# Carrying a part of the rows of a column roll through SBUF beside HBM to HBM copies

## The chip, the cores and the metric

The kernel runs on one core of a Trainium2 chip. The metric is the device time of one execution in microseconds (us): a median of 828.96 us over 3 runs (828.69 to 829.57) before the change. One further execution was taken with the hardware profiler; its span, from the first to the last instruction, is 815.4 us, and its own time is 817.17 us.

## What is computed

```python
def setup_inputs():
    return {"x": np.random.randn(8192, 8192).astype(np.float32), "shift": 100}

def reference(x, shift):
    return np.roll(x, shift, axis=1)
```

Every row of 8192 floats (32,768 B) is shifted right by 100 columns. The last 100 values of a row, its wrapped end, come to stand at the front of the same row. Nothing is calculated: 268 MB are read from the chip's memory (HBM) and 268 MB are written to it.

## The kernel before, in words

With shift 100 the kernel has `s = 100`, `a = 128` (the shift rounded up to 128 columns, so that writes start at a multiple of 512 B) and `g = a - s = 28`. It cuts every output row into two parts.

The **body** is columns 128 to 8191 of the output, 8064 values or 32,256 B of each row, which are columns 28 to 8091 of the input. It is copied straight from HBM to HBM by 16 DMA instructions (lines 30 to 37). The views `xm` and `om` order the rows as (c, e, j): e has 16 values, one for each DMA engine, and j has 4. Each instruction takes one j and a quarter of the c values, that is 32 x 16 rows or 16.5 MB; one packet is one row of 32,256 B. The instructions go in turn to two DMA rings, that of the Sync engine (SP) and that of ScalarE (ACT).

The **ends** are columns 0 to 127 of the output: 100 wrapped values and the first 28 values of the input row. [...]lines 54 to 76 build them in SBUF. In each of two groups of 4096 rows, three DMA instructions on the GpSimd (POOL) queue (line 67) read 128 values across each row boundary (the end of one row and the start of the next lie side by side in memory), two more fetch what the boundaries inside the group don't give (lines 68 and 71), and VectorE (DVE) sorts the values into whole 512 B ends with two copies (lines 69 and 72). Four DMA instructions (line 76) then store the ends. All loads of both groups are issued before the first store: the stores stand in a loop of their own.

Within one engine's queue, instructions are issued one after the other. Tile, the layer that the kernel is written in, orders the instructions and sets the semaphores between them. The pools `reads` and `heads` have a buffer for each group, so no load waits for a store.

The 16 body copies wait for no data. The only thing that holds them back is how many may be under way.

Of the kernel before, what the change touches and what calls it, by code (L numbers as in the profile page):

```python
# [1 line left out]

# [4 lines left out]


@with_exitstack
def kernel(  # L10
    ctx: ExitStack,
    tc: tile.TileContext,
    x: bass.AP,
    shift: int,
    out: bass.AP,
):
    nc = tc.nc
    n_rows, n_cols = x.shape
    s = shift % n_cols
    a = -(-s // 128) * 128  # L20
    g = a - s
    P = nc.NUM_PARTITIONS
    engines = [nc.sync, nc.scalar]
    n_chunks = 16
    rows = n_rows // n_chunks

    xm = x.rearrange("(c e j) w -> j e c w", e=16, j=4)  # L30
    om = out.rearrange("(c e j) w -> j e c w", e=16, j=4)
    depth = n_rows // 64 // 4
    for c in range(4):
        for j in range(4):
            if a < n_cols:
                cs = slice(c * depth, (c + 1) * depth)
                engines[j % 2].dma_start(out=om[j, :, cs, a:], in_=xm[j, :, cs, g:n_cols - s])
    if a == 0:
        return


    if a > 512:
        for i in range(n_chunks):
            r = slice(i * rows, (i + 1) * rows)
            nc.gpsimd.dma_start(out=out[r, :s], in_=x[r, n_cols - s:])
            if g > 0:
                nc.gpsimd.dma_start(out=out[r, s:a], in_=x[r, :g])
        return

    Q, J = 4, 8
    n_st = n_rows // (P * Q * J)
    reads = ctx.enter_context(tc.tile_pool(name="reads", bufs=n_st))
    heads = ctx.enter_context(tc.tile_pool(name="heads", bufs=n_st))
    xt = x.rearrange("(k p j q) c -> k q p j c", q=Q, j=J, p=P)
    ot = out.rearrange("(k p j q) c -> k q p j c", q=Q, j=J, p=P)
    tiles = []  # L60
    for k in range(n_st):
        t = reads.tile([P, Q - 1, J, a], x.dtype)
        h = heads.tile([P, Q, J, a], x.dtype)
        for q in range(1, Q):
            lead = bass.AP(tensor=x.tensor, offset=(k * P * J * Q + q) * n_cols - s,
                           ap=[[J * Q * n_cols, P], [Q * n_cols, J], [1, a]])
            nc.gpsimd.dma_start(out=t[:, q - 1], in_=lead)  # L67
        nc.gpsimd.dma_start(out=h[:, Q - 1, :, :s], in_=xt[k, Q - 1, :, :, n_cols - s:])  # L68
        nc.vector.tensor_copy(h[:, :Q - 1, :, :s], t[:, :, :, :s])  # L69
        if g > 0:  # L70
            nc.gpsimd.dma_start(out=h[:, 0, :, s:], in_=xt[k, 0, :, :, :g])  # L71
            nc.vector.tensor_copy(h[:, 1:, :, s:], t[:, :, :, s:])  # L72
        tiles.append(h)
    for k, h in enumerate(tiles):
        for q in range(Q):
            nc.gpsimd.dma_start(out=ot[k, q, :, :, :a], in_=h[:, q])  # L76


# [1 line left out]
_INS = ['x', 'shift']  # L80
_OUTS = [((8192, 8192), 'float32')]

_NUMBERS = {'shift': 100}


# [26 lines left out]
```

## Time and profile before

| What | Value |
|---|---|
| Median time | 828.96 us |
| Span of the profiled execution | 815.4 us |
| VectorE busy | 3.7 us in 4 instructions |
| GpSimd busy | 16.1 us in 22 instructions |
| Body copies | 16 instructions of 16,128 KB, median 401.3 us (SP) and 400.5 us (ACT) from issue to landing |
| Loads for the ends | 6 of 512 KB, 118.2 us to landing; 2 of 400 KB, 151.3 us; 2 of 112 KB, 146.1 us |
| Stores of the ends | 8 of 512 KB, 182.5 us to landing |
| Last stores of the ends issued | 241.7 us |

How to read it: the time to landing of a DMA counts from its issue, so a copy that stands behind three others in its ring has a long one without being slow itself. The profile gives the DMA engines' busy share and the bytes that they moved in each stretch of the span. It counts a copy from HBM to HBM once in its GB/s, although HBM both reads and writes those bytes; for the total of HBM, reads and writes are added. A stretched packet counts as busy time, so a share of 1.00 does not tell whether the engines move data at their full rate.

### The profile page before, as it was taken

The numbers are of one execution on the slowest core, as the hardware profiler recorded it, in microseconds if no ns is written. First come the engines' busy times: TensorE is split into PE (matmuls) and PEld (weight loads), VectorE is DVE, ScalarE is ACT, GpSimd is POOL, SyncE is SP. The second block draws the span as 40 slices with busy tenths as digits, with TensorE's granted clock in tenths as the row PEclk, the third lists the DMA queues.
The fourth block names the chain that finished last, engine by engine and source line by source line (L and its number), as shares of the span: only waits on it lengthen the run. The fifth ranks groups of instructions, "written<-read, shape, count | busy, mean of one in ns | idle before, by whom it ended". The sixth has DMA issues, their size and how long they took to land. (4 is left out here: it accounts for less than half of the span.)

```text
span 815.4 us, 93 instructions
## 1 busy us (share of the span) xinstructions
DVE 3.7 (0%) x4; POOL 16.1 (2%) x22
## 2 busy tenths in 40 slices
DVE  0000000000000000000000000000000000000000
POOL 3000001000010000000000000000000000000000
DMA  9999999999999999999999999999999999999996
GB/s 310 341 328 347 330 349 335 337 340 346 338 337 346 338 348 348 347 333 345 340 344 337 349 326 335 334 329 334 335 329 331 329 335 334 332 331 332 329 334 250
DMA packets 10784, 272.63 MB, mean 334 GB/s; under 512 B 544, under 2 KB 544, under 8 KB 2592
## 3 DMA queue, kind: packets, MB, share of 16 engines
q10 hardware_dynamic: 4224, 132.12, 47.0%
q1 hardware_dynamic: 4224, 132.12, 46.9%
q0 software_dynamic: 2336, 8.39, 4.5%
HBM read 268.44 MB, written 268.44 MB: 658 GB/s over the span
## 5 line engine op out<-in xcount | busy, mean ns | idle before, releaser
L76 POOL DMA_DIRECT2D out_dram<-h x8 | 6.9, 954 | 170.1 <-DMA h<-in_x_dram 144.1
L67 POOL DMA_DIRECT2D t<-in_x_dram x6 | 5.4, 910 | 0.8 <-PEq L107 0.8
L69 DVE COPY h<-t 128x2400 f32<-128x2400 f32 x2 | 2.8, 1410 | 208.5 <-DMA t<-in_x_dram 208.5
L71 POOL DMA_DIRECT2D h<-in_x_dram x2 | 1.8, 883 | 28.6 <-DMA t<-in_x_dram 28.6
L68 POOL DMA_DIRECT2D h<-in_x_dram x2 | 1.8, 882 | 27.0 <-DMA t<-in_x_dram 27.0
L72 DVE COPY h<-t 128x672 f32<-128x672 f32 x2 | 1.0, 503 | 0.0
L93 POOL MEMSET const-float32-0.0<- 128x1 f32 x1 | 0.1, 99 | 0.2 <-issue 0.2
L93 POOL MEMSET const-bfloat16-1.0<- 128x1 bf16 x1 | 0.1, 103 | 0.0
L93 POOL MEMSET const-float32-1.0<- 128x1 f32 x1 | 0.1, 99 | 0.0
L93 POOL MEMSET const-uint8-127<- 128x1 uint8 x1 | 0.1, 99 | 0.0
## 6 DMA issues: line engine op xcount, KB each, us to landing
out_dram<-in_x_dram SPq DMA_DIRECT2D x8, 16128.0 KB, 401.3
out_dram<-in_x_dram ACTq DMA_DIRECT2D x8, 16128.0 KB, 400.5
out_dram<-h POOLq DMA_DIRECT2D x8, 512.0 KB, 182.5
t<-in_x_dram POOLq DMA_DIRECT2D x6, 512.0 KB, 118.2
h<-in_x_dram POOLq DMA_DIRECT2D x2, 400.0 KB, 151.3
h<-in_x_dram POOLq DMA_DIRECT2D x2, 112.0 KB, 146.1
```

The lines of the kernel that those rows point to most:

```text
L67: nc.gpsimd.dma_start(out=t[:, q - 1], in_=lead)
L68: nc.gpsimd.dma_start(out=h[:, Q - 1, :, :s], in_=xt[k, Q - 1, :, :, n_cols - s:])
L69: nc.vector.tensor_copy(h[:, :Q - 1, :, :s], t[:, :, :, :s])
L71: nc.gpsimd.dma_start(out=h[:, 0, :, s:], in_=xt[k, 0, :, :, :g])
L72: nc.vector.tensor_copy(h[:, 1:, :, s:], t[:, :, :, s:])
L76: nc.gpsimd.dma_start(out=ot[k, q, :, :, :a], in_=h[:, q])
L93: nc = _bacc.Bacc("TRN2", target_bir_lowering=False, num_devices=1)
```

## The change

The rows are divided. The last 1536 rows (3 batches of 128 partitions with 4 rows each) no longer take the copy and the ends. Each batch is loaded whole into SBUF, 4 rows or 131,072 B in a partition, at an offset of 100 values. VectorE then moves each row's last 100 values to the place in front of that row: four copies of 128x100 values for a batch. Because the rows lie side by side, the place in front of a row is where the end of the row before it stood, which has been moved by then. After that, one store from the start of the buffer writes the rolled rows. Loads and stores go on ACT's ring, cut into blocks of 16 KB. The pool `rows` has one buffer, so the batches follow one another.

The other 6656 rows keep the body copies, now all on SP's ring: 16 instructions of 26 x 16 rows each. Their ends are built as before, in two groups of 4096 and 2560 rows (J = 8 and 5), but each group's stores now stand right behind its own loads in the program text, and the batches' loads, copies and stores stand ahead of everything else.

What it is for: part of the traffic takes a way on which reads and writes go through SBUF as separate transfers on a ring of their own, and whose ends cost no short packets.

```diff
-    engines = [nc.sync, nc.scalar]
-    n_chunks = 16
-    rows = n_rows // n_chunks
+    per = 4
+    batches = 3
+    top = n_rows - batches * P * per
...
-    xm = x.rearrange("(c e j) w -> j e c w", e=16, j=4)
-    om = out.rearrange("(c e j) w -> j e c w", e=16, j=4)
-    depth = n_rows // 64 // 4
-    for c in range(4):
-        for j in range(4):
-            if a < n_cols:
-                cs = slice(c * depth, (c + 1) * depth)
-                engines[j % 2].dma_start(out=om[j, :, cs, a:], in_=xm[j, :, cs, g:n_cols - s])
+    pool = ctx.enter_context(tc.tile_pool(name="rows", bufs=1))
+    W = per * n_cols
+
+    def load(b):
+        r = slice(top + b * P * per, top + (b + 1) * P * per)
+        t = pool.tile([P, W + s], x.dtype)
+        nc.scalar.dma_start(out=t[:, s:], in_=x[r].rearrange("(p j) c -> p (j c)", j=per),
+                            max_dma_last_dim=16384)
+        return t
+
+    def store(b, t):
+        r = slice(top + b * P * per, top + (b + 1) * P * per)
+        for j in range(per):
+            if s > 0:
+                nc.vector.tensor_copy(t[:, j * n_cols:j * n_cols + s], t[:, (j + 1) * n_cols:(j + 1) * n_cols + s])
+        nc.scalar.dma_start(out=out[r].rearrange("(p j) c -> p (j c)", j=per), in_=t[:, :W],
+                            max_dma_last_dim=16384)
+
+    for b in range(batches):
+        store(b, load(b))
...
+    xm = x[:top].rearrange("(c e j) w -> j e c w", e=16, j=4)
+    om = out[:top].rearrange("(c e j) w -> j e c w", e=16, j=4)
+    if a < n_cols:
+        for c in range(0, top // 64, 26):
+            for j in range(4):
+                nc.sync.dma_start(out=om[j, :, c:c + 26, a:], in_=xm[j, :, c:c + 26, g:n_cols - s])
...
-    Q, J = 4, 8
-    n_st = n_rows // (P * Q * J)
-    reads = ctx.enter_context(tc.tile_pool(name="reads", bufs=n_st))
-    heads = ctx.enter_context(tc.tile_pool(name="heads", bufs=n_st))
...
-    for k in range(n_st):
...
+    Q = 4
+    reads = ctx.enter_context(tc.tile_pool(name="reads", bufs=1))
+    heads = ctx.enter_context(tc.tile_pool(name="heads", bufs=1))
+    r0 = 0
+    for k, J in enumerate((8, top // (P * Q) - 8)):
+        R = P * Q * J
...
-        tiles.append(h)
-    for k, h in enumerate(tiles):
         for q in range(Q):
-            nc.gpsimd.dma_start(out=ot[k, q, :, :, :a], in_=h[:, q])
+            nc.gpsimd.dma_start(out=ot[q, :, :, :a], in_=h[:, q])
+        r0 += R
```

The branch for shifts above 512 columns also changes, but isn't taken here.

More of the change, by code (lines that the diff above doesn't have):

```diff
@@ L42 @@
     if a > 512:
-        for i in range(n_chunks):
-            r = slice(i * rows, (i + 1) * rows)
-            nc.gpsimd.dma_start(out=out[r, :s], in_=x[r, n_cols - s:])
+        for r0 in range(0, top, 512):
+            nc.gpsimd.dma_start(out=out[r0:r0 + 512, :s], in_=x[r0:r0 + 512, n_cols - s:])
             if g > 0:
-                nc.gpsimd.dma_start(out=out[r, s:a], in_=x[r, :g])
+                nc.gpsimd.dma_start(out=out[r0:r0 + 512, s:a], in_=x[r0:r0 + 512, :g])
         return
-    Q, J = 4, 8
@@ L55 @@
-    n_st = n_rows // (P * Q * J)
-    reads = ctx.enter_context(tc.tile_pool(name="reads", bufs=n_st))
-    heads = ctx.enter_context(tc.tile_pool(name="heads", bufs=n_st))
-    xt = x.rearrange("(k p j q) c -> k q p j c", q=Q, j=J, p=P)
-    ot = out.rearrange("(k p j q) c -> k q p j c", q=Q, j=J, p=P)
-    tiles = []
-    for k in range(n_st):
-        t = reads.tile([P, Q - 1, J, a], x.dtype)
-        h = heads.tile([P, Q, J, a], x.dtype)
+    Q = 4
+    reads = ctx.enter_context(tc.tile_pool(name="reads", bufs=1))
@@ L64 @@
+    heads = ctx.enter_context(tc.tile_pool(name="heads", bufs=1))
+    r0 = 0
+    for k, J in enumerate((8, top // (P * Q) - 8)):
+        R = P * Q * J
+        xt = x[r0:r0 + R].rearrange("(p j q) c -> q p j c", q=Q, j=J)
+        ot = out[r0:r0 + R].rearrange("(p j q) c -> q p j c", q=Q, j=J)
+        t = reads.tile([P, Q - 1, J, a], x.dtype, name=f"t{k}")
+        h = heads.tile([P, Q, J, a], x.dtype, name=f"h{k}")
         for q in range(1, Q):
-            lead = bass.AP(tensor=x.tensor, offset=(k * P * J * Q + q) * n_cols - s,
+            lead = bass.AP(tensor=x.tensor, offset=(r0 + q) * n_cols - s,
@@ L66 @@
                            ap=[[J * Q * n_cols, P], [Q * n_cols, J], [1, a]])
             nc.gpsimd.dma_start(out=t[:, q - 1], in_=lead)
-        nc.gpsimd.dma_start(out=h[:, Q - 1, :, :s], in_=xt[k, Q - 1, :, :, n_cols - s:])
+        nc.gpsimd.dma_start(out=h[:, Q - 1, :, :s], in_=xt[Q - 1, :, :, n_cols - s:])
         nc.vector.tensor_copy(h[:, :Q - 1, :, :s], t[:, :, :, :s])
         if g > 0:
-            nc.gpsimd.dma_start(out=h[:, 0, :, s:], in_=xt[k, 0, :, :, :g])
+            nc.gpsimd.dma_start(out=h[:, 0, :, s:], in_=xt[0, :, :, :g])
```

## The prediction

> **What bounds the kernel now.** I read the page first (engines, slices, DMA queues), then the stretches of the span by windows, then the waits of the DMA queues.
>
> ```profile
> DVE 3.7 (0%) x4; POOL 16.1 (2%) x22
> DMA  9999999999999999999999999999999999999996
> DMA packets 10784, 272.63 MB, mean 334 GB/s; under 512 B 544, under 2 KB 544, under 8 KB 2592
> q10 hardware_dynamic: 4224, 132.12, 47.0%
> q1 hardware_dynamic: 4224, 132.12, 46.9%
> q0 software_dynamic: 2336, 8.39, 4.5%
> HBM read 268.44 MB, written 268.44 MB: 658 GB/s over the span
> ```
>
> No compute engine matters: VectorE works 3.7 us of 815.4. The DMA engines are busy in every slice until the last, and the two big queues share them evenly. That looks like "the DMA engines are the bound", but busy is not the same as fast. The mean copy packet lasts 0.47 x 815.4 x 16 / 4096 = 1.50 us for 32,256 B, while the shortest in the trace's packet records lasts 1.19 us, that is 27.1 GB/s for one engine and 433 GB/s for 16. The packets are stretched by a quarter, by something behind the engines. The windows tell what:
>
> ```profile
> core 0: us, DVE busy (x) POOL busy (x), PEclk, DMA share, GB/s
> 250.00:420.00 170.00, 0.00 (x0) 0.00 (x0) 1.00 1.00 343
> 440.00:600.00 160.00, 0.00 (x0) 0.00 (x0) 1.00 1.00 334
> 600.00:750.00 150.00, 0.00 (x0) 0.00 (x0) 1.00 1.00 332
> 757.00:796.00 39.00, 0.00 (x0) 0.00 (x0) 1.00 0.94 336
> 801.60:806.80 5.20, 0.00 (x0) 0.00 (x0) 1.00 0.77 329
> ```
>
> A copy from HBM to HBM costs the memory two bytes for each byte moved. From 440 to 750 us only copies run and HBM moves 2 x 333 = 666 GB/s. From 757 one engine has finished: 15 engines, share 0.94, still 2 x 336 = 672. From 801.6 four are idle, share 0.77, and HBM still moves 658, with the packets near full speed. Taking a sixteenth or a quarter of the engines away costs nothing or 1%. So HBM's read and write total of about 666 GB/s is the bound, and the engines have slack behind it. At 666, the 536.9 MB need 806.1 us; the span is 815.4, so start, ends traffic and the uneven finish of the engines cost 9.3 us.
>
> ```profile
> SPq L37 <- DMA out_dram<-in_x_dram: 47.6, 4, 16.7
> 0.74 496.05 SPq L37 DMA_DIRECT2D out_dram<-in_x_dram  x8
> ```
>
> In SP's own waits and in its timeline the fifth to eighth copy each wait for an earlier copy. The records give the 16 copies eight completion semaphores, handed out in turn to both rings; a copy waits until the last owner of its semaphore has landed. That costs nothing now; it matters for the change.
>
> **What the Trainium skill says.** "DMA: Bandwidth & Descriptors", section Specifications, gives a ceiling of 435 GB/s for the 16 engines; the 433 from the shortest packet agrees. "HBM Reference", section Specifications (TRN2), gives about 716 GB/s for the memory that two cores share; the trace's 666 is 93% of it, and nothing here shows whether the rest can be had. "DMA: Bandwidth & Descriptors", section Queues, rings and completion order, says that each engine takes turns between its queues packet by packet; 46.9% and 47.0% for the two queues agree. The same page, section Issuing engines are not separate DMA queues, says that the issuing engine brings no DMA engine of its own; here too both rings land on the same 16.
>
> **The change part by part.**
>
> *Bytes at HBM.* Every row is still read once and written once, the carried rows with 32,768 B each way, the others with 32,256 B and their ends. HBM's 536.9 MB stay. At the same rate this part is 0 us.
>
> *Work for the DMA engines.* Copies: 6656 x 32,256 B = 214.7 MB (before 264.2). Carried rows: 1536 x 32,768 B x 2 = 100.7 MB, since a load and a store each pass an engine. Ends: 8.39 x 6656/8192 = 6.8 MB. Sum 322.2 MB, up 18%. At 433 GB/s the engines need 744 us (before 630). So the demand that they can put on HBM falls from 536.9/630 = 852 to 536.9/744 = 722 GB/s: still above 666, but by 8% and no longer by 28%.
>
> *What HBM gives at that demand.* The windows bracket it: 0.94 x 866 = 814 of demand gave 672, and 0.77 x 866 = 667 gave 658 (866 is 2 x 433). At 722 I take 662, between the two and a little below the plateau. 536.9/662 = 811.0 us, 4.9 more than before. Bounds: 640 (838.9 us) if load and store phases fluctuate, 690 (778.1 us) if carrying rows lets HBM do better.
>
> *How the rings run together.* A packet of 32,256 B alternates with one of 16,384 B. An engine has 416 SP packets (6656/16) and 6 x 64 = 384 on ACT's ring. At one to one ACT's chain (load, copy, store, three times, in one buffer of 131.5 KB a partition) would end after 384 of SP's packets. At its five inner waits SP runs alone and HBM stays full. Each wait lasts some 10 us: the slowest engine, the landing, the VectorE copies. That is about 7 SP packets, so ACT ends near packet 419 of 416. The two end together; I charge 1 us.
>
> *The copies on VectorE.* The rows of VectorE's copies in the page's part 5 give (1410 - 503)/(2400 - 672) = 0.525 ns per element and 150 ns fixed, so 128x100 takes 0.20 us, four take 0.8 us, twelve 2.4 us. They delay only ACT's store, while SP's packets fill the engines: 0 us.
>
> *Loads, stores and their waits.* ACT's second load waits for the first store to have been read out of the buffer. Behind it on ACT's queue stand only its own later transfers, and SP fills the time: 0 us.
>
> *Ends on the POOL queue.* 19% fewer, in two groups, the second one smaller. Now each group's stores are issued before the next group's loads. Before, all was landed by about 440 us, so there is room for a longer chain: 0 us as long as VectorE does the ends' copies early (see the last rival).
>
> *Edges.* The same 9.3 us. Sum: 811.0 + 9.3 + 1 = 821 us of span, 5.9 more than now. The time is 828.96 - 815.4 = 13.6 us above the profile's span, which gives 834.9; rounded down for the slightly shorter ends traffic, 834 us, 0.6% slower.
>
> **The rivals.**
>
> *HBM gives more (faster).* Half of each copy's cost may be reads and writes of the same row disturbing each other; carried rows read and write at different times. For it: from 250 to 420 us, where stores from SBUF run beside the copies, HBM moves (343 x 2 - 19) = 667, a touch above the later 664; and in the packet records all stores of ends take the same 0.16 us for 4 KB, never stretched, while loads of ends stretch to 0.46 us on average. The waiting is on the read side, and a sixth of the engines' time would now go to stores that do not wait. Against it: the rise is 0.5%, and fewer reading engines did not raise the total. At 690: 778.1 + 9.3 + 13.6 = 801 us; at 680, 812 us.
>
> *The engines become the bound (slower).* If 722 of demand against 666 of supply already rubs, HBM gets 640: 838.9 + 9.3 + 13.6 = 862 us. For it: demand and supply are within 8%. Against it: at a demand of 667, 658 was reached.
>
> *The order of the semaphores or of VectorE holds a ring (slower).* If the eight semaphores are handed out in the order of the program text, ACT's six transfers own the first six, and SP's third to eighth copy each wait for one of them. Then two copies (53.7 MB at HBM) and the first load take about 110 us, the next five steps of one copy and one transfer some 77 us each (51 mixed, 23 with the transfer alone at the engines' 433 GB/s, 3 of waits), and the last nine copies (241.6 MB) 363 us: 858 us, with edges and offset about 881. If SP's 16 copies come first instead, ACT's store waits for SP's ninth copy, and the carried rows' last two transfers run alone at half of HBM's rate: about 858. Third, if the twelve row copies stand ahead of the ends' copies on VectorE, the ends' stores and the second group begin only when the last load has landed, at five sixths of the span (680 us); 4.7 MB at 19 to 30 GB/s then take 157 to 247 us, up to 940 us in time. Against all three: the records give ACT's copy the lower semaphore of each pair although SP's stands first in the text, so the order is not the text's but follows readiness, and the ends' loads land long before a 16.8 MB load.
>
> **How the numbers follow.** The plateau case, 822 to 846 us: chance 0.42. HBM gives more, 795 to 822: 0.35. Engines the bound, near 862: 0.11. An order that holds a ring, 858 to 940: 0.12. The likeliest gives 834. The low edge, 798, leaves the best of the second case out; the high edge, 870, takes in the engines' case and the milder order. Faster by over 0.2%: 0.35 and a part of the plateau case's lower end, 0.42; same 0.12; slower 0.46.
>
> **What would show it.** Right: HBM near 660 GB/s over mixed stretches, DMA near 395 GB/s, share 1.00; the two rings ending within some 10 us of each other; VectorE row copies near 0.20 us; SP without long waits. Wrong: mixed stretches at 680 or more (the second case), a DMA total near 385 with all engines busy (the third), or slices in which DMA moves near 433 and HBM the same, which is ACT alone, or ends that land last (the fourth).

## The result, and the profile after

The changed kernel takes 885.81 us (median of 4 runs, 884.97 to 887.02) against 828.83 us for the kernel before (827.04 to 829.57 in 4 runs): 1.069 times as long, 95% interval 1.067 to 1.071. It is 57 us slower, where 5 us were forecast.

One caution on reading. The kernel before took 828.8 us here and 820.8, 833.1 and 831.6 us in the three comparisons below, which ran on three different chips, each on one occasion; its profiled execution, shown ahead of the prediction, took 817.17 us. So the level goes with the chip or the occasion, and the runs don't tell which. The ratios of the experiments are always within one chip. Times and GB/s of different comparisons can differ by up to 2% with no change in the kernel.

The page of the changed kernel, the lines that answer to those of before:

```profile
DVE 5.9 (1%) x16; POOL 15.6 (2%) x22
DMA  9999999999899989999998999999999999999998
GB/s 364 402 393 401 406 352 361 405 399 391 377 363 386 407 350 389 399 433 362 390 407 351 387 396 432 309 330 315 338 325 333 324 334 331 331 327 328 331 328 280
DMA packets 15120, 322.18 MB, mean 364 GB/s; under 512 B 656, under 2 KB 656, under 8 KB 2320
q1 hardware_dynamic: 6912, 214.70, 67.4%
q10 hardware_dynamic: 6240, 100.66, 27.8%
HBM read 268.44 MB, written 268.44 MB: 607 GB/s over the span
```

The bytes are as worked out beforehand: 322.18 MB through the DMA engines, 268.44 MB each way at HBM. HBM's mean is what fell, from 658 to 607 GB/s, although the DMA engines are still busy in every slice. The GB/s row shows two kernels in one: up to slice 25 it swings between 350 and 433, and from there to the end it stays near 330. The swing is the thing to follow. ACT's ring is q10, SP's is q1. The windows of the changed kernel (length, VectorE and GpSimd busy, clock, DMA share, GB/s):

```profile
core 0: us, DVE busy (x) POOL busy (x), PEclk, DMA share, GB/s
250.00:285.00 35.00, 0.00 (x0) 0.00 (x0) 1.00 1.00 397
375.00:398.00 23.00, 0.00 (x0) 0.00 (x0) 1.00 1.01 432
532.00:553.00 21.00, 0.00 (x0) 0.00 (x0) 1.00 1.01 434
560.00:860.00 300.00, 0.00 (x0) 0.00 (x0) 1.00 1.00 330
```

From 560 us on only SP's copies run: 330 GB/s, 660 at HBM, the plateau. From 250 to 285 both rings run: 397 GB/s, of which the packet records give 265 to copies, so HBM moves 662; in the later mixed stretches it moves 653 to 659. But from 375 to 398 and from 532 to 553 the 432 and 434 GB/s come from ACT's ring alone. A load or a store passes HBM once, so HBM moves 432 and a third of it is unused. The highest DMA figures of the profile are its worst stretches. In the packet records SP's ring, once started, holds less than a tenth of the engines for 128 us of the first 554. At 430 instead of 658 GB/s that costs, as an estimate, 128 x (1 - 430/658) = 44 us.

Why SP stands still is in the waits of its DMA queue and in ACT's timeline (start, length and instruction):

```profile
SPq L61 <- DMA t<-in_x_dram: 274.4, 3, 120.4
SPq L61 <- DMA out_dram<-t: 274.1, 3, 120.3
```

```profile
0.74 0.42 ACTq L38 DMA_DIRECT2D t<-in_x_dram  x1
139.56 0.39 ACTq L47 DMA_DIRECT2D out_dram<-t  x1
244.39 0.40 ACTq L38 DMA_DIRECT2D t<-in_x_dram  x1
323.08 0.38 ACTq L47 DMA_DIRECT2D out_dram<-t  x1
399.33 0.40 ACTq L38 DMA_DIRECT2D t<-in_x_dram  x1
477.96 0.38 ACTq L47 DMA_DIRECT2D out_dram<-t  x1
```

SP's copies, line 61, wait six times for loads and stores of carried rows: 548 us, with which they have no data in common. The records of the instructions name the completion semaphore of each transfer, and with it the reason:

```
semaphore   first owner           later owner (waits for the first)
107         ACT load 1            SP copy 3    issued at 122.5 us
108         SP copy 1             SP copy 4              123.1
110         ACT store 1           SP copy 5              244.4
111         ACT load 2            SP copy 6              322.0
112         ACT store 2           SP copy 7              399.3
113         ACT load 3            SP copy 8              476.9
114         ACT store 3           SP copy 9              554.5
115         SP copy 2             SP copy 10             555.1
```

There are eight semaphores for both rings, and each goes to its next owner in turn. ACT's six transfers have six of the first eight. From copy 5 on, one copy of SP is let in for each ACT transfer that lands. A copy of 13.4 MB lands 53 to 57 us after its issue, the transfer beside it lasts 76 to 78, and for the rest of the step ACT is alone. (Copies 4 and 10 follow a copy of SP that had landed long before, and don't wait.) After store 3 has landed at 554 us, the remaining 8 copies run freely, but nothing is left to run beside them.

### The profile page after: what moved, and what is told of

The parts are those of the page before. It is cut to its first block, busy times and chain, and to the rows that moved or that the text cites. A ratio compares the mean times of both kernels' runs of the same rounds, so it can differ in the third digit from the quotient of the medians.

```text
span 884.4 us, 116 instructions
## 1 busy us (share of the span) xinstructions
DVE 5.9 (1%) x16; POOL 15.6 (2%) x22
## 2 busy tenths in 40 slices
DMA packets 15120, 322.18 MB, mean 364 GB/s; under 512 B 656, under 2 KB 656, under 8 KB 2320
## 3 DMA queue, kind: packets, MB, share of 16 engines
HBM read 268.44 MB, written 268.44 MB: 607 GB/s over the span
## 4 chain that ended last, share of the span: by engine, by line
another core or an unknown queue 47%; DMA 6%; DVE 1%; POOL 0%; issue 0%; DVEq 0%
DMA t<-in_x_dram 6%; POOL out_dram L97 0%; DVE t L46 0%; DVE h L92 0%; DVE h L95 0%; POOL t L90 0%; DVEq L46 0%; DVEq L92 0%
## 5 line engine op out<-in xcount | busy, mean ns | idle before, releaser
L46 DVE COPY t<-t 128x100 f32<-128x100 f32 x12 | 2.8, 237 | 336.8 <-DMA t<-in_x_dram 336.5
L92 DVE COPY h<-t 128x2400 f32<-128x2400 f32 (+1 forms) x2 | 2.4, 1202 | 135.2 <-DMA t<-in_x_dram 135.2
## 6 DMA issues: line engine op xcount, KB each, us to landing
t<-in_x_dram ACTq DMA_DIRECT2D x3, 16384.0 KB, 77.6
```

The costliest lines, as they stand in the source:

```text
L46: nc.vector.tensor_copy(t[:, j * n_cols:j * n_cols + s], t[:, (j + 1) * n_cols:(j + 1) * n_cols + s])
```

## The experiments

The theory (A in the expectations): the shared semaphores hold SP back, and apart from that the change would cost about 1%. Rivals: the mixed traffic is slow by itself (B); carrying rows brings HBM something that the hold hides (C). The runs with 8, 32 and 4 copies and with one batch share one chip; the two that follow them, the one with a single ring and the one with rows side by side share a second; the run with both copies moved on VectorE and the two that leave traffic out share a third. In the expectations, e5 is the run with the semaphores in another order, and e6 the first try at VectorE's order. Many expectations also name microseconds. These were worked out at the level of an earlier comparison, so for several runs they are off by that difference alone; the ratio to the kernel before on the same chip is what tests the theories.

**Half as many copies, twice as long.** The copies are the same rows in 8 instructions, so that each time SP waits, the copy that it issued before is still under way.

```diff
-        for c in range(0, top // 64, 26):
+        for c in range(0, top // 64, 52):
...
-                nc.sync.dma_start(out=om[j, :, c:c + 26, a:], in_=xm[j, :, c:c + 26, g:n_cols - s])
+                nc.sync.dma_start(out=om[j, :, c:c + 52, a:], in_=xm[j, :, c:c + 52, g:n_cols - s])
```

> The changed kernel with SP's body in 8 copies of 52 x 16 rows instead of 16 of 26 x 16; nothing else differs. Theory A (shared completion semaphores hold SP): each copy is long enough that the ACT transfer whose semaphore it needs has landed before SP gets there, so SP never stands still; ACT's six transfers always run beside copies, HBM stays at 650 to 660 GB/s, 536.9 MB / 0.652 = 823 us plus some 9 of edges: span about 832, time 826 to 846. Theory B (the mixed traffic itself is slow, the semaphores don't matter): within 1% of the changed kernel, 877 to 894. Theory C (without the hold HBM gives 680 or more): 790 to 812.

825.98 us, 1.0064 of the kernel before (1.004 to 1.0088). The 57 us are gone but for 5. The page, the windows and SP's waits of this run:

```profile
GB/s 371 389 406 402 410 416 360 345 347 402 408 400 391 404 405 362 392 402 397 403 400 379 401 396 409 401 406 393 376 404 391 400 397 397 322 404 406 392 406 349
HBM read 268.44 MB, written 268.44 MB: 652 GB/s over the span
400.00:500.00 100.00, 0.85 (x4) 0.00 (x0) 1.00 1.00 396
500.00:600.00 100.00, 0.00 (x0) 0.00 (x0) 1.00 1.01 396
600.00:700.00 100.00, 0.00 (x0) 0.00 (x0) 1.00 1.00 397
SPq L61 <- DMA t<-in_x_dram: 387.9, 3, 130.1
SPq L61 <- DMA out_dram<-t: 278.2, 2, 147.2
```

No slice reaches 430, and none but the one near 700 us falls below 345: the rings stay together, and ACT ends 8.5 us after SP. At 396 GB/s the packet records give 270 to copies and 126 to carried rows, so HBM moves 666; from 600 to 700 it is 660. Yet SP's waits for loads and stores of carried rows have not gone: with 666 us in total they are longer than the 548 of the changed kernel. What has gone is the empty ring. When each of the last four waits ends, the copy ahead still has 95, 65, 32 and 2 us to run by the landing times, so the room is nearly used up. A wait of the queue that issues costs nothing as long as its ring has work. The engines carry 19% more bytes than with plain copies (333 GB/s in the next run, on this chip), and HBM about the same.

**Twice as many copies, half as long.** The same edit with 13 in place of 26, 32 copies.

> The changed kernel with SP's body in 32 copies of 13 x 16 rows. Theory A: each hold lets only one or two half-size copies pass for each ACT transfer, so more of ACT's bytes run alone: the six transfers end at about 421 us, 9 of 32 copies are done by then, and the other 23 (154 MB, 309 MB at HBM) take 469 us at 658 GB/s: span about 894, time 890 to 905, slower than the changed kernel. Theory B: the size of the copies doesn't matter, 877 to 894, like the changed kernel.

898.83 us, ratio 1.0956 (1.0938 to 1.0974). It was expected at 890 to 905 by the theory and at 877 to 894 by the rival. Its windows show both parts of the picture:

```profile
145.00:170.00 25.00, 0.00 (x0) 0.00 (x0) 1.00 1.00 429
400.00:425.00 25.00, 0.00 (x0) 0.00 (x0) 1.00 1.00 431
430.00:600.00 170.00, 0.00 (x0) 0.00 (x0) 1.00 1.00 333
600.00:850.00 250.00, 0.00 (x0) 0.00 (x0) 1.00 1.00 332
```

SP's ring is below a tenth for 191 us here, by the same count as above (128 in the changed kernel, some 10 in the run with 8 copies, nearly all at its end). At 430 of 665 GB/s, 191 us cost an estimated 67 us; the run stands 73 us above the one with 8 copies. The time follows how long SP's ring stands empty, not the number of bytes.

**Four copies.** The same edit with 104. SP then waits for no ACT transfer but the first load.

> The changed kernel with SP's body in 4 copies of 104 x 16 rows, so that ten transfers share the eight semaphores and the only ACT transfer that SP waits for is the first load, which lands long before it is needed. Theory A: the same as with 8 copies within 0.7%, 824 to 846. Theory B: 877 to 894. If a long copy has a price of its own, it stands above the run with 8 copies.

828.61 us, ratio 1.0088 (1.0068 to 1.0107): level with 8 copies within the intervals. The size of a copy has no price of its own that can be told here.

**One batch instead of three**, with 8 copies of 60 x 16 rows: `batches = 1`, and 60 in place of 26.

> One batch of 512 rows carried instead of three, SP's body in 8 copies of 60 x 16 rows; SP waits for no ACT transfer before it has landed. Theory A with a constant HBM rate: the carried rows cost nothing and gain nothing, 826 to 838, and a little faster than three batches if the mixed stretch (652 GB/s in the changed kernel) is a bit below the plain copies (658). Theory C: a third of the gain of three batches, 815 to 823.

820.60 us, ratio 1.0005 (0.9994 to 1.0017). In microseconds this lies in rival C's range and below theory A's; but the kernel before took 820.80 us on this chip, so it is no gain. A third of the carried rows costs nothing and gains nothing. With three batches and SP's ring never long empty it is 0.6 to 0.9%: rival C finds nothing, and carrying rows becomes dearer, not cheaper, as more are carried.

**The same 16 copies, semaphores in another order.** This changes which copy waits for which transfer, and leaves every transfer as it is in the changed kernel. The text gives load, three copies, store, two copies, and so on, and each ACT transfer but the first is tied in order, without a wait, behind the copy ahead of it.

```diff
...
-    for b in range(batches):
-        store(b, load(b))
...
+    last = None
+    for b in range(batches):
+        t = load(b, last)
+        last = copies(3)
+        store(b, t, last)
+        last = copies(2)
+    copies(1)
...
```

Here `copies(n)` issues SP's next n copies, and `load` and `store` call `tc.add_manual_dep(..., NoSync, ...)` from their transfer to `last`.

> The changed kernel with the same 16 copies of 26 x 16 rows and the same six transfers on ACT's ring, but the program text gives them in turn (load, three copies, store, two copies, and so on), with an order but no wait between the rings, so that the eight semaphores are handed out in that order: where SP's copy shares one with an ACT transfer, that transfer has landed some two copies earlier. Theory A (the shared semaphores hold SP and nothing else is wrong): as with 8 copies, 1.000 to 1.010 of the kernel before, 820 to 830. Theory B2 (the holds come from the number or size of the copies, not from whose semaphore they share): as the changed kernel, 1.05 to 1.08, 865 to 885.

840.46 us, ratio 1.0091 (1.0056 to 1.0126). It is the cleanest of the tests: same transfers, same sizes, same rings, another order in which eight semaphores are handed out, and SP's ring no longer runs empty. One thing moves besides: the first store is issued at 184 us instead of 140; the run with both copies moved on VectorE, below, brings it back to 131 at the same ratio, so this is not what helped. The windows are even, and SP's queue still waits for ACT's transfers, 337 us in all, but with at least one copy still under way:

```profile
300.00:400.00 100.00, 0.00 (x0) 0.00 (x0) 1.00 1.00 386
400.00:500.00 100.00, 0.85 (x4) 0.00 (x0) 1.00 1.00 388
500.00:600.00 100.00, 0.00 (x0) 0.00 (x0) 1.00 1.00 382
600.00:700.00 100.00, 0.00 (x0) 0.00 (x0) 1.00 1.00 392
SPq L64 <- DMA out_dram<-t: 178.5, 2, 91.6
SPq L64 <- DMA t<-in_x_dram: 158.4, 2, 111.3
```

**VectorE's order, a first try.** In the runs with 8, 4 and 16 reordered copies the first store is issued only at 184 to 186 us, although its load landed by 130 to 133: the row copies stand behind VectorE's copies for the second group of ends.

> As the run before it in this list, and VectorE's copies of the second group of ends stand behind the first batch's four row copies instead of ahead of them. In the run with 8 copies the first store waited until 184 us for them although its load had landed by 130, and ACT ended 9 us after SP. Theory A: ACT ends 40 to 50 us earlier, before SP, and SP alone keeps HBM full at the end: 0 to 5 us less than without it, 816 to 825, at most level with the kernel before since HBM's bytes and rate are the same. If carrying rows brings HBM anything, it shows here: below 0.99.

841.04 us, ratio 1.0088 (1.0059 to 1.0116). The edit missed its aim: it moved the 100-wide copy of the ends and left the 28-wide one ahead, which waits for the same loads, and the first store was issued at 182 us. The run says nothing on the question.

**VectorE's order, both copies moved** behind the first batch's row copies:

> The turn-by-turn order of e5, and both of VectorE's copies for the second group of ends stand behind the first batch's four row copies (in e6 only one of the two did, and the first store was issued at 182 us as before). Theory A: the first store is issued near 132 us, ACT's ring ends some 50 us earlier and well before SP's, and what ACT did alone at the end (3 to 4 us at a lower HBM rate) is gone: ratio to the kernel before 1.003 to 1.008, the rest being mixed stretches in which HBM moves 1% less than with plain copies. Rival: carrying rows gains once ACT is out of the way, ratio below 0.998.

838.38 us, ratio 1.0081 (1.0054 to 1.0109), at the top of what was expected. Now the edit took. VectorE's timeline between 100 and 200 us, and ACT's first two rows:

```profile
129.61 0.95 DVE L52 COPY t<-t 128x100 f32<-128x100 f32 x4 [65.02 <-DMA t<-in_x_dram]
194.06 0.99 DVE L104 COPY h<-t 128x1500 f32<-128x1500 f32 x1 [63.51 <-DMA t<-in_x_dram]
```

```profile
0.74 0.42 ACTq L44 DMA_DIRECT2D t<-in_x_dram  x1
130.59 0.39 ACTq L53 DMA_DIRECT2D out_dram<-t  x1
```

The store starts 53 us earlier, ACT's ring is done at 800 us instead of 839, and the ratio stays where it was, within the intervals. The wait on VectorE's queue was real and cost nothing measurable, since SP's copies ran meanwhile. The rival of a hidden gain is not seen. What remains of 0.8% fits the mixed stretches, though no run isolates it: from 300 to 780 us the packet records give HBM 647 to 653 GB/s in this run, and 658 to the plain copies of the run without row stores, on the same chip.

**One ring for the copies of the kernel before**: `engines = [nc.sync, nc.sync]`.

> The kernel before with all 16 body copies on SP's ring. If one ring alone moves less than two (after 560 us the changed kernel's SP ring moved 330 GB/s by itself, the kernel before 333), the time rises by about 1%, 826 to 832, and a part of the loss of the changed kernel is the lost second ring. If the ring does not matter, 819 to 823.

831.74 us, ratio 0.9986 (0.9972 to 1.0). The copies alone move this much on that chip with one ring:

```profile
440.00:600.00 160.00, 0.00 (x0) 0.00 (x0) 1.00 0.99 327
600.00:750.00 150.00, 0.00 (x0) 0.00 (x0) 1.00 1.00 327
```

It is 2% under the 333 of the first profile, and in microseconds the run lies where a lost ring was expected to put it. Yet the kernel before, with two rings, took 833.14 us on this chip: the time is level, and the lower rate is no effect of the ring. The lost second ring is no part of the loss.

**Rows side by side**: in the kernel before, `"(c j e) w -> j e c w"` in place of `"(c e j) w -> j e c w"`.

> The kernel before with the rows of a copy dealt so that the 16 engines read 16 rows that lie side by side, 32 KB apart, where now they are 128 KB apart. If HBM's 666 GB/s depends on how far apart the engines' rows are, the time moves by more than 0.5%, either way; if it is a limit of the total, 819 to 823.

834.18 us, ratio 1.0005 (0.9991 to 1.0019). Whether the engines' rows lie 32 or 128 KB apart makes no difference.

**What the limit is: without the row stores, and without the row loads.** Two kernels of the kind with the semaphores in turn leave out one half of the carried rows' traffic (2 runs each).

> e5 with the three stores of carried rows left out (1536 rows of the output stay unwritten); loads and row copies remain. HBM reads 268.4 MB as always and writes 218.1 instead of 268.4. If the limit is the total of reads and writes: 486.6 MB / 0.655 to 0.666 = 731 to 743 us, and 11 of edges: ratio 0.895 to 0.91. If it is a limit on reads alone: ratio 0.99 to 1.01. If on writes alone: 0.82 to 0.83.

> e5 with the three loads and the row copies left out; the stores write a buffer that VectorE has filled with zeros (1536 rows of the output are zero). HBM writes 268.4 MB and reads 218.1. Total of reads and writes as the limit: ratio 0.895 to 0.91, as without the stores. Reads alone: 0.82 to 0.83. Writes alone: 0.99 to 1.01.

755.36 us, ratio 0.9071 (0.9033 to 0.9109), and 762.15 us, ratio 0.9152 (0.9117 to 0.9188). HBM's bytes fell to 486.6/536.9 = 0.906 in both. A limit on reads alone would have left the first at 1 and brought the second to 0.82, one on writes the reverse. Both are ruled out; the limit is near the sum. Whether it sits in the memory itself or on the way to it, these runs don't tell. The second stands 0.5% above the expected 0.91. In it the stores start only when VectorE has filled the buffer, at 35 us, and while they run, up to 495 us, the packet records give HBM 637 to 651 GB/s, a little less than beside loads (652 to 653 in the other run); the reason was not tried.

No version that was run beats the kernel before. Nothing here points to one that would carry rows: without the empty ring the result lies between level (one batch) and 0.9% slower (three). A second row buffer and other block sizes were not tried.

## Why the prediction was wrong

The direction was right, at a chance of 0.46, and the size was not: 834 us forecast, 885.8 measured, above the high edge of 870.

- **What bounds the kernel: right.** HBM's sum of reads and writes is the limit, shown by the two runs that leave out a half of the carried traffic.
- **Bytes, engines' load: right.** 322.2 MB and 536.9 MB are on the page.
- **What HBM gives at the lower demand: right in size, in part by luck.** The step put 662 against a plateau of 666, 0.6% less. Where SP's ring is not empty the mixed stretches show 647 to 653 GB/s against 658 for plain copies on one chip, 639 to 653 against 650 to 656 on another, and mostly 654 to 667 against 663 to 667 on the third (one stretch 645); the times are 0.6 to 0.9% above the kernel before. But the lower end of the bracket was misread. The view counts the packets that start in a window, and in one of 5.2 us that is too many: 12 of 16 engines are at work, and it says 0.77. Spread over their time the packets give 318 GB/s, so HBM moved 636 and not 658, near what 12 engines can carry (0.75 x 866 = 650). With 15 engines the same count gives 666, so that part of the reading holds. Put right, the bracket would have given about 649 at a demand of 722 (an estimate), 2.5% under the plateau.
- **How the rings run together: this step failed.** It let SP's packets and ACT's alternate to the end, counted waits of ACT alone ("SP runs alone and HBM stays full") and charged 1 us. The alternation is right where both rings have work: from 250 to 285 us, 8.2 packets of SP and 8.0 of ACT start in a microsecond. (The equal shares of the two queues before, which the prediction put beside it, follow already from their equal bytes.) What it had wrong is that SP always has a packet ready; the step on loads, stores and their waits, 0 us because "SP fills the time", fell with it. In the profile ACT ends at 554 us and SP at 883, and SP is out for 128 us of the first 554. The runs put its price at 1.0692/1.0091, or 6% of the time: some 49 us of the 57, where the step had 1.
- **The semaphores: seen, and set aside on a wrong inference.** The prediction named this hold as a rival, worked it out at 881 us, and gave the whole group of order rivals a chance of 0.12. Against it stood one observation: in the kernel before, ACT's copy of each pair has the lower semaphore although SP's comes first in the text, so the order follows readiness. The observation is true, and in the changed kernel too ACT's load has the lower one of the first pair. It does not lead to the conclusion: in the changed kernel all six ACT transfers got their semaphores before SP's second copy, although five of them wait for an earlier transfer and that copy for none. So the order follows neither the text alone nor readiness at run time. What it follows stays open; with copies half as long SP's second copy came ahead of two ACT transfers (semaphore 113), which would fit an order by expected durations, but no run tests that. The rival's steps were close where they could be checked: SP's issues at 244.4, 322.0, 399.3, 476.9 and 554.5 us are 77.3 to 77.6 us apart, and 77 was worked out; it had nine copies left at the end where there were eight, and too little for the first two transfers (187 us, where it took 244).
- **VectorE's copies: right in cost, and the wait behind the ends was not foreseen.** The page has 237 ns for a row copy, 200 were expected. The first load had landed by 122 us and the store went out at 139.6, since the ends' copies stood ahead. Moving them, in a kernel whose SP ring stays filled, showed no gain.
- **Ends on the POOL queue: right.** The last packet of their stores lands at 201 us; no transfer waits for them.
- **The 13.6 us between span and time: mislabelled.** A profiled execution's time is 1.8 us above its span, before (817.17 and 815.4) and after (886.22 and 884.4). The rest of the 13.6 lies between the profiled execution and the timed runs, and is of the size seen between chips; the record names no chip for either, so its cause is not shown. It did little harm here, since 834 was compared with timed runs.

## What to carry to other kernels

When two DMA rings draw on one set of completion semaphores, list which transfer owns which semaphore before believing that the rings are independent: a chain of dependent transfers on one ring can become the clock of the other, though they share no data. Look at whether the ring runs empty, not at how long its queue waits: 666 us of waits cost next to nothing in the run with 8 copies, and 548 us went with a loss of 6% in the changed kernel. Read GB/s together with what each byte costs at the memory, for the highest DMA rate of this profile was its worst stretch. And where HBM's sum of reads and writes is the limit, as here, don't expect time from a detour through SBUF: it gave the DMA engines 18% more bytes, and the runs stood between level and 0.9% slower as long as no overlap was lost.

## What had not been expected of the hardware

The same kernel takes 820.8 to 833.1 us on different chips (one occasion each), and the plain copies' rate moves with it (333 to 327 GB/s); a rate from one chip compared with a rate from another would have shown a loss of 1 to 2% that isn't there. The limit on HBM hardly depends on how it is reached: one ring or two, rows 32 or 128 KB apart, plain copies or copies beside carried rows, all come to 637 to 667 GB/s of reads and writes. Loads or stores alone between HBM and SBUF run at 426 to 434 GB/s. There nearly every packet of 16 KB takes 611 to 622 ns, close to the shortest of the trace, and 16 engines at 611 ns make 429 GB/s: here the engines are the limit.
